# A decoder layer's two down projections, from plain k-tile sums to Strassen products

## The chip, the cores and the metric

One core of one Trainium2 chip runs the whole program in one launch. The time is the device time of one execution in microseconds (us); several runs give a median.

The engines, as the profile names them: PE is TensorE's matmuls (PEld its weight loads), DVE is VectorE, ACT is ScalarE, POOL is GpSimd, SP is SyncE, which here only issues DMAs. Each has its own queue and works through it in order; they wait for one another by semaphores. PE writes to PSUM, whose tiles DVE and ACT read; all else lies in SBUF or in DRAM.

## What is computed

One layer of a hybrid decoder for 1024 prompt and 64 sample positions, 1088 columns in all, width 1024, in fp32:

```
x = x + 1/2 * SwiGLU_1(rmsnorm(x))
h = rmsnorm(x);  z = h @ w_in
... three mixing branches (windowed attention, a recurrence, memory attention) ...
x = x + merged @ w_out
x = x + 1/2 * SwiGLU_2(rmsnorm(x))
y = rmsnorm(x)

def swiglu(x, w_gu, w_down):                 # d_model 1024, d_ff 2816
    gate, up = split(x @ w_gu, 2)
    return (silu(gate) * up) @ w_down
```

The change concerns the product with `w_down` in both SwiGLU blocks: 2816 x 1024 weights against 1088 columns.

## The kernel before

**Layout.** Everything is kept transposed: a tile has 128 rows (channels) and positions as its columns. d_ff is 22 k-tiles of 128 (`KF`), d_model 8 tiles (`KD`). The 1088 columns are taken either in three chunks of 352, 368 and 368 (`CH`), or in two halves (`tp`) of 544, each of two blocks of 272 columns (`TC`).

**A product in three matmuls.** Each fp32 operand is split into a coarse part and a rest (both fp32r). `mac3` (L262 to L264) issues three matmuls for each k-tile: coarse x coarse, coarse x rest, rest x coarse.

**Weights.** A plan (`make_plan`) lists all weight tiles in the order of use. `load` (L154) has SP fetch the next one, 128 x 1024 (512 KB), into one of four raw buffers (`wr`). `part` splits 128 x 512 of it: ACT copies the coarse part (L167), DVE subtracts it from the raw tile (L168). Seven split tiles (`ws`, `RING`) are the ring between them and PE. `ahead`, called inside `mac3`, has the next ones made as ring places come free.

**Gate stage** (`gate_up`). The up and gate products of a k-tile pair are Strassen's already (`quad`, `combined`): seven products of 272 columns, with sums of weight blocks on DVE and POOL (L183) and the results put together by `swiglu` (DVE L539, POOL L557, L561 and L506). The hidden tiles, silu(gate) x up, go to DRAM (`h_d`). The last two k-tiles (`ALONE`) are done for one half, then for the other; in between, `change` frees the first half's operands and starts the down stage's loads: `first_hidden` loads and splits hidden tiles 0 to 3, and in stage 1 `fetch_x` (L1654) loads the residual x straight into the accumulator.

**Down stage** (`down`, `down_tile`). The 22 k-tiles go in eleven pairs. For each pair, eight output tiles o times three chunks are six matmuls each into one PSUM bank; DVE adds the bank to the accumulator x in SBUF (L648). In stage 2 the first pair is copied by ACT (L646), and the residual is loaded and added to x by POOL (L1822) during the second pair. Hidden tiles are fetched by SP (L569) and split by ACT (L573, which also scales by 1/2) and DVE (L574). In the last pair the loop runs over the chunks outside, and `after` does each finished tile's share of what comes next: norm sums (L321), in stage 1 the split operands of the next product (L281, L282), in stage 2 the final norm.

The order of the instructions on each engine is the order in which the program issues them, as a scheduler lays them out; `tick` and `later` spread work of DVE, ACT and POOL between PE's tiles.

## Time and profile before

| | us |
|---|---|
| runs (3): median, lowest to highest | 2748.35, 2745.88 to 2750.64 |
| the profiled execution | 2746.11 |
| its span, first to last instruction | 2744.3 |
| TensorE's mean granted clock | 0.989 of full speed |
| PE, DVE, ACT, POOL busy | 2658.8, 1728.8, 910.3, 834.4 |
| matmuls of the down stages | 3168 |

The down stage of the first SwiGLU lies at 515 to 780 us of the span, that of the second at 2455 to 2723. Matmul records overlap their neighbours (a matmul's mean duration is longer than the distance to the next one's start), so a rate of PE is read from starts in a window. A few records can be missing.

### The profile page before, as it was taken

Reading aid. Unit: us, or ns where it says so; the run is one execution under the profiler, and the core shown is the slowest. Engines: PE = TensorE matmul, PEld = TensorE weight load, DVE = VectorE, ACT = ScalarE, POOL = GpSimd, SP = SyncE. Lnnn points to the kernel's source line nnn. Section 1 sums busy time; section 2 is a strip of 40 time slices with the busy share of each in tenths; the row PEclk is TensorE's granted clock in tenths of the full one; section 3 lists DMA queues with packets and bytes.
Section 4 is the critical chain, followed back from the end, with each engine's and each line's share of the span. In section 5 each row is a group of like instructions: output and inputs, shape, how many; then the busy total and the mean of one; then the engine's idle time right before and its main releaser. Section 6 shows DMA issues by size and latency. Waiting matters only on the chain.

```text
span 2744.3 us, 46291 instructions
## 1 busy us (share of the span) xinstructions
PE 2658.8 (97%) x18088; PEld 2578.8 (94%) x18088; DVE 1728.8 (63%) x3032; ACT 910.3 (33%) x1747; POOL 834.4 (30%) x751
## 2 busy tenths in 40 slices
PE   7999999999999999999989999999999999999997
PEld 7999999899999899989978889999999999999997
DVE  7766566777774433546577755863766666576776
ACT  6332323311153312323334543422542232242112
POOL 2365555200030000324353411231225555553003
PEclk9999999999999999999999999999999999999998
DMA  4222323522243342655544442754424455445221
GB/s 150 70 94 84 103 99 108 206 96 92 76 166 126 96 148 75 208 181 159 174 156 136 138 134 94 262 178 164 149 98 176 163 186 189 168 157 173 96 73 66
DMA packets 181403, 374.98 MB, mean 137 GB/s; under 512 B 21768, under 2 KB 116168, under 8 KB 180416
## 3 DMA queue, kind: packets, MB, share of 16 engines
q1 hardware_dynamic: 166464, 303.85, 33.7%
q0 software_dynamic: 2048, 43.65, 4.7%
q10 hardware_dynamic: 12672, 24.52, 2.4%
q8 instruction: 142, 2.33, 0.4%
q14 instruction: 77, 0.63, 0.1%
HBM read 305.59 MB, written 113.16 MB: 153 GB/s over the span
## 4 chain that ended last, share of the span: by engine, by line
PE 83%; DVE 10%; ACT 2%; issue 2%; DMA 2%; POOL 1%; SPq 0%; DVEq 0%; ACTq 0%; POOLq 0%
PE pg L262 9%; PE pg L264 9%; PE pg L263 9%; PE z L262 7%; PE z L263 7%; PE z L264 7%; PE pd L262 6%; PE pd L263 6%; PE pd L264 6%; DVE ws L168 2%; PE po L264 2%; PE po L263 2%; PE po L262 2%; PE o L814 1%; PE wo L262 1%
## 5 line engine op out<-in xcount | busy, mean ns | idle before, releaser
L262 PE MATMUL pg<-xo,ws 128*128 128x272 f32 x2512 | 730.3, 291 | 18.6 <-DVE uu L539 10.6
L264 PE MATMUL pg<-xo,ws 128*128 128x272 f32 x2512 | 727.0, 289 | 5.2 <-DVE ws L168 5.2
L263 PE MATMUL pg<-xo,ws 128*128 128x272 f32 x2512 | 726.7, 289 | 0.0
L167 ACT ACTIVATE ws<-wr 128x512 fp32r<-128x512 f32 (+1 forms) x550 | 324.9, 613 | 839.9 <-PE pd L264 363.9
L168 DVE TENSOR_TENSOR ws<-wr,ws 128x512 fp32r<-128x512 f32 (+1 forms) x550 | 439.4, 822 | 133.7 <-ACT ws L167 133.3
L262 PEld LDWEIGHTS pg<-xo,ws 128*128 128x128 f32 x2512 | 476.5, 190 | 21.3 <-DVE uu L539 12.8
L264 PEld LDWEIGHTS pg<-xo,ws 128*128 128x128 f32 x2512 | 476.4, 190 | 5.8 <-DVE ws L168 5.8
L262 PE MATMUL z<-xg,ws 128*128 128x368 f32 (+1 forms) x1392 | 478.9, 344 | 0.0
L263 PEld LDWEIGHTS pg<-xo,ws 128*128 128x128 f32 x2512 | 476.8, 190 | 0.0
L264 PE MATMUL z<-xg,ws 128*128 128x368 f32 (+1 forms) x1392 | 460.2, 331 | 0.0
L263 PE MATMUL z<-xg,ws 128*128 128x368 f32 (+1 forms) x1392 | 459.8, 330 | 0.0
L262 PE MATMUL pd<-h,ws 128*128 128x368 f32 (+1 forms) x1056 | 348.7, 330 | 3.7 <-DVE x L648 2.6
L263 PE MATMUL pd<-h,ws 128*128 128x368 f32 (+1 forms) x1056 | 346.8, 328 | 0.0
L264 PE MATMUL pd<-h,ws 128*128 128x368 f32 (+1 forms) x1056 | 345.9, 328 | 0.0
L648 DVE TENSOR_TENSOR x<-x,pd 128x368 f32<-128x368 f32 (+1 forms) x504 | 258.0, 530 | 137.6 <-PE pd L264 133.8
L262 PEld LDWEIGHTS z<-xg,ws 128*128 128x128 f32 x1392 | 265.2, 191 | 15.7 <-issue 14.2
L263 PEld LDWEIGHTS z<-xg,ws 128*128 128x128 f32 x1392 | 265.5, 191 | 1.4 <-issue 0.2
L264 PEld LDWEIGHTS z<-xg,ws 128*128 128x128 f32 x1392 | 264.1, 190 | 0.0
L262 PEld LDWEIGHTS pd<-h,ws 128*128 128x128 f32 x1056 | 199.3, 189 | 4.3 <-DVE x L648 2.9
L264 PEld LDWEIGHTS pd<-h,ws 128*128 128x128 f32 x1056 | 199.4, 189 | 0.0
L263 PEld LDWEIGHTS pd<-h,ws 128*128 128x128 f32 x1056 | 199.4, 189 | 0.0
L978 POOL TENSOR_TENSOR qb<-qb,kv 128x1024 f32<-128x1024 f32 x48 | 116.2, 2424 | 198.0 <-DMA qb<-qs_d 146.6
(297 smaller groups left out, 3705.0 us busy)
## 6 DMA issues: line engine op xcount, KB each, us to landing
wr<-in_w_gu_dram SPq DMA_DIRECT2D x96, 512.0 KB
wr<-in_w_in_dram SPq DMA_DIRECT2D x58, 512.0 KB
qb<-qs_d SPq DMA_DIRECT2D x48, 512.0 KB
h_d<-sl ACTq DMA_DIRECT2D x88, 272.0 KB
hr<-h_d SPq DMA_DIRECT2D x44, 544.0 KB
wr<-in_w_dn_dram SPq DMA_DIRECT2D x44, 512.0 KB
out_sk_dram<-in_cache_k_dram POOLq DMA_DIRECT2D x16, 1020.0 KB, 6.9
out_sv_dram<-in_cache_v_dram POOLq DMA_DIRECT2D x16, 1020.0 KB, 8.3
```

The lines of the kernel that those rows point to most:

```text
L167: nc.scalar.activation(spl[:, 0, :n], src, AF.Copy)
L168: nc.vector.tensor_tensor(out=spl[:, 1, :n], in0=src, in1=spl[:, 0, :n].bitcast(F32), op=OP.subtract)
L262: nc.tensor.matmul(out, wh, xh, start=start and i == 0, stop=False, **more)
L263: nc.tensor.matmul(out, wh, xl, start=False, stop=False, **more)
L264: nc.tensor.matmul(out, wl, xh, start=False, stop=i == n - 1, **more)
L648: nc.vector.tensor_tensor(out=xa, in0=xa, in1=ps[:, :n], op=OP.add)
L814: nc.tensor.matmul(po[:, e], pt[:, h, j * 128:(j + 1) * 128], z["vt"][:, kb[j], e], start=j == 0, stop=j == len(kb) - 1)
L978: nc.gpsimd.tensor_tensor(out=prev, in0=prev, in1=kk, op=OP.mult)
```

## The change

Twenty of the 22 k-tiles of each down stage are done in five groups of four (`DGROUPS`). A group is a 2 x 2 by 2 x 2 block product: weights in blocks of two k-tiles by four output tiles, hidden tiles in blocks of two k-tiles by 272 columns of both halves. Strassen's scheme (in Winograd's form) makes seven products of it, in the order `DOPS`.

- `downed` makes the split weights of the seven products, two tiles for each, from four raw tiles held at once. Sums of weight blocks are formed in place on POOL (L221 to L230 of the new file).
- `hidden_operand` splits an operand of 4 x 272 columns for each product (ACT, DVE L603) and forms sums of hidden blocks in place on POOL (L627). It is called two products ahead. `load_hidden` fetches two k-tiles in one DMA (L613).
- `down_groups` runs over 35 products. A product is four output tiles; each has 12 matmuls into a PSUM tile of two banks (544 columns in use), four of which exist. `sum_product` adds that tile to the product's own sum: products 5, 2, 4 and 3 straight in x, products 1, 6 and 7 in three further tiles (`sum`). In the first group ACT copies products 1, 5, 6 and 7; in products 6 and 2 (`DASIDE`) of all groups but the last, unless copied so, ACT copies the tile to SBUF (`et`) and POOL adds it (L736); all else is DVE's (L738).
- In the last group the seven sums are combined once, tile by tile, by DVE and POOL (`ends`, L686), in SBUF.
- The residual is loaded into x ahead of the first group in both stages (`residual`), but for one block of columns that product 5 writes first; that block comes apart (`late`) and is added in the last group.
- The last two k-tiles are left as they were (`down`); their hidden tiles are loaded and split during the last group.
- Weights of `w_down` come in plain rows, one k-tile of 128 x 1024 in each load.

```diff
-DOWN = [(k, 2, 512) for k in range(0, KF - 2, 2)] + [(KF - 2, 2, 1024)]
+DGROUPS = (KF - 2) // 4
+DOPS = (1, 5, 7, 6, 2, 4, 3)
+DASIDE = (6, 2)
...
+    def downed(self, name, raws):
+        tt = self.nc.gpsimd.tensor_tensor
+        blocks = [[r[:, a:a + 512] for r in (raws[q], raws[2 + q]) for a in (0, 512)] for q in range(2)]
...
+        for m in DOPS:
+            for q, (a11, a21, a12, a22) in enumerate(blocks):
+                put(m, q, {1: a11, 5: a21, 7: a11, 6: a11, 2: a12, 4: a22, 3: a12}[m])
+                if m == 1:
+                    if q == 0:
+                        tt(out=a11, in0=a11, in1=a21, op=OP.subtract)
+                    else:
+                        tt(out=blocks[0][1], in0=blocks[0][1], in1=blocks[0][3], op=OP.add)
+                        tt(out=a11, in0=a11, in1=a21, op=OP.subtract)
+                if (m, q) == (5, 0):
+                    tt(out=blocks[1][1], in0=blocks[1][1], in1=blocks[1][3], op=OP.add)
+                if m == 7:
+                    tt(out=a11, in0=a22, in1=a11, op=OP.subtract)
+                if m == 2:
+                    tt(out=a12, in0=a12, in1=a11, op=OP.subtract)
+                if q and m in (2, 3):
+                    self.load()
+                    self.load()
+                yield
...
+    def hidden_operand(self, n):
+        group, idx = divmod(n, 7)
...
+        self.split_hidden(self.hop[n], {1: b11, 5: b11, 7: b12, 6: b11, 2: b21, 4: b21, 3: b22}[m])
...
+        if m == 1:
+            less(b11, b12, b11)
+        if m == 5:
+            less(b12, b22, b12)
+        if m == 7:
+            less(b11, b22, b11)
+        if m == 2:
+            less(b21, b21, b11)
+            self.load_hidden(group + 1, 0)
+        if m == 3:
+            self.load_hidden(group + 1, 1)
...
-    def down(self, dn, pool, raws, after, residual=None):
-        for g, (k, nk, w) in enumerate(DOWN):
...
+    def down_groups(self, dn, sums, extra, src, last):
...
+        acc = {1: s1, 6: s6, 7: s7, 5: x11, 2: x00, 4: x10, 3: x01}
+        ends = {1: ((nc.vector, s6, s1), (nc.gpsimd, x00, s1)), 2: ((nc.gpsimd, x01, x11),),
+                3: ((nc.vector, x11, s7), (nc.gpsimd, x10, s7)), 4: ((nc.gpsimd, x11, "late"), (nc.vector, x01, s6)),
+                5: ((nc.vector, x10, s6),), 6: ((nc.gpsimd, x11, s6),)}
+        for n in range(7 * DGROUPS):
...
+            for o in range(4):
+                ps = self.bank("s", "pd")
+                for tp in range(2):
+                    self.mac3(ps[:, tp * 512:tp * 512 + TC],
+                              [(tuple(w[:, s, o * 128:(o + 1) * 128] for s in range(2)),
+                                (xo[:, 0, 2 * q + tp], xo[:, 1, 2 * q + tp])) for q, w in enumerate(ws)], steps=False)
+                self.sum_product(group, m, acc[m][o], ps.rearrange("p (t n) -> p t n", t=2)[:, :, :TC], end, extra)
+                if end:
+                    for eng, out, x in ends.get(idx, ()):
+                        tt(eng, out[o], late[:, o] if x == "late" else x[o])
+                if o < 2:
+                    if len(self.ready) + self.using < RING:
+                        self.make()
+                if o == 2:
+                    self.hidden_operand(n + 2)
...
+    def sum_product(self, group, m, acc, ps, end, extra):
+        nc = self.nc
+        if group == 0 and m in (1, 5, 6, 7):
+            nc.scalar.activation(acc, ps, AF.Copy)
+        elif m in DASIDE and not end:
+            t = extra("et")
+            nc.scalar.activation(t, ps, AF.Copy)
+            nc.gpsimd.tensor_tensor(out=acc, in0=acc, in1=t, op=OP.add)
+        else:
+            nc.vector.tensor_tensor(out=acc, in0=acc, in1=ps, op=OP.add)
```

What stands where, at three places. First DVE in the middle of the down stage 1 (`x` and `sum` are accumulators, `pd` is PSUM, `ws` split weights, `ho` a product's split hidden operand). Before:

```order
L648 TENSOR_TENSOR x_5535<-x_5535,pd_6165 128x352
L648 TENSOR_TENSOR x_5535<-x_5535,pd_6181 128x368
L648 TENSOR_TENSOR x_5535<-x_5535,pd_6189 128x368
L648 TENSOR_TENSOR x_5535<-x_5535,pd_6197 128x352
L648 TENSOR_TENSOR x_5535<-x_5535,pd_6205 128x368
```

After, in a middle group:

```order
L738 TENSOR_TENSOR x_5535<-x_5535,pd_7253 128x2x272
L171 TENSOR_TENSOR ws_7267<-wr_6978,ws_7267 128x512
L738 TENSOR_TENSOR x_5535<-x_5535,pd_7270 128x2x272
L171 TENSOR_TENSOR ws_7284<-wr_6976,ws_7284 128x512
L738 TENSOR_TENSOR x_5535<-x_5535,pd_7288 128x2x272
L603 SCALAR_TENSOR_TENSOR ho_7302<-hr_7015,ho_7302 128x1088
L738 TENSOR_TENSOR x_5535<-x_5535,pd_7306 128x2x272
```

and in the last group, with a combining sum (L686) behind each PSUM sum:

```order
L738 TENSOR_TENSOR x_5535<-x_5535,pd_7891 128x2x272
L686 TENSOR_TENSOR sum_5845<-sum_5845,sum_5844 128x544
L171 TENSOR_TENSOR ws_7907<-wr_7473,ws_7907 128x512
L738 TENSOR_TENSOR x_5535<-x_5535,pd_7910 128x2x272
L686 TENSOR_TENSOR sum_5845<-sum_5845,sum_5844 128x544
```

A product's four sums now alternate with two weight splits and one operand split; before, the splits of a pair stood between 24 sums.

Second POOL in stage 1. Before, nothing stands between the gate stage's last products and the norm sums of the last pair:

```order
L557 TENSOR_TENSOR uu_5747<-uu_5747,rbc 128x544
L506 TENSOR_TENSOR sl_5787<-sl_5787,uu_5747 128x544
L321 TENSOR_TENSOR acc_8038<-acc_8038,td_8052 128x352
```

After, from a middle group's product 2 on (`et` is ACT's copy of a PSUM tile, `wr` raw weights, `hr` raw hidden tiles):

```order
L736 TENSOR_TENSOR x_5535<-x_5535,et_7117 128x2x272
L736 TENSOR_TENSOR x_5535<-x_5535,et_7140 128x2x272
L221 TENSOR_TENSOR wr_6976<-wr_6976 128x512
L736 TENSOR_TENSOR x_5535<-x_5535,et_7160 128x2x272
L736 TENSOR_TENSOR x_5535<-x_5535,et_7181 128x2x272
L223 TENSOR_TENSOR wr_6976<-wr_6976,wr_7123 128x512
L224 TENSOR_TENSOR wr_6978<-wr_6978 128x512
L226 TENSOR_TENSOR wr_6978<-wr_6978,wr_7125 128x512
L627 TENSOR_TENSOR hr_7015<-hr_7015 128x4x272
```

Four more such L736 rows stand right ahead; the weight sums of the next group, L223 among them, stand behind all eight.

Third SP's queue at the opening of stage 1. Before:

```order
L154 DMA wr_5580<-in_w_dn_dram 128x1024
L569 DMA hr_5536<-h_d 128x1088
L569 DMA hr_5538<-h_d 128x1088
L154 DMA wr_5582<-in_w_dn_dram 128x1024
L1654 DMA x_5535<-in_x_dram 128x1088 x8
L569 DMA hr_5686<-h_d 128x1088
L154 DMA wr_5725<-in_w_dn_dram 128x1024
```

After:

```order
L157 DMA wr_5586<-in_w_dn_dram 128x1024
L613 DMA hr_5542<-h_d 128x2x1088
L613 DMA hr_5544<-h_d 128x2x1088
L157 DMA wr_5588<-in_w_dn_dram 128x1024
L681 DMA x_5535<-in_x_dram 128x1088 x4
L679 DMA x_5535<-in_x_dram 128x2x272 x4
L157 DMA wr_5724<-in_w_dn_dram 128x1024
L157 DMA wr_5726<-in_w_dn_dram 128x1024
L679 DMA late_7815<-in_x_dram 128x2x272 x4
```

All four hidden tiles of the first group now stand ahead of x, and the third and fourth weight tile behind it.

## Rows read from the trace of the kernel before

**Rows 1.** The page, busy us (share of the span), instructions of each engine.

```profile
PE 2658.8 (97%) x18088; PEld 2578.8 (94%) x18088; DVE 1728.8 (63%) x3032; ACT 910.3 (33%) x1747; POOL 834.4 (30%) x751
```

**Rows 2.** Windows: length, then PE, PEld, DVE, ACT, POOL busy, clock, DMA, GB/s.

```profile
560.00:720.00 160.00, 160.00 (x977) 160.00 (x976) 113.79 (x203) 30.18 (x42) 0.00 (x0) 1.00 0.27 89
350.00:400.00 50.00, 50.00 (x402) 50.00 (x401) 29.54 (x50) 13.68 (x24) 26.52 (x22) 1.00 0.23 79
480.00:502.00 22.00, 19.19 (x149) 18.53 (x148) 21.88 (x30) 10.21 (x17) 12.12 (x8) 1.00 0.66 254
```

**Rows 3.** The tile pd: durations min/median/max in ns, one of three matmul lines.

```profile
L262 PE MATMUL pd<-h,ws x1056: 317/330/508, 515.7 to 2722.4; 128*128 128x352 f32 x166, 128*128 128x368 f32 x10
```

**Rows 4.** Groups by line and shape, DVE, 520 to 760 us: busy us, mean ns.

```profile
L648 DVE TENSOR_TENSOR x<-x,pd 128x368 f32<-128x368 f32 x160 | 84.9, 537 | 50.4 <-PE pd L264 50.4
L648 DVE TENSOR_TENSOR x<-x,pd 128x352 f32<-128x352 f32 x85 | 44.0, 519 | 16.9 <-PE pd L264 16.9
L168 DVE TENSOR_TENSOR ws<-wr,ws 128x512 fp32r<-128x512 f32 x41 | 26.4, 685 | 3.3 <-ACT ws L167 3.3
L574 DVE SCALAR_TENSOR_TENSOR h<-hr,h 128x1088 fp32r<-128x1088 f32 x18 | 23.1, 1284 | 0.0
```

**Rows 5.** The same view, DVE, gate stage, 200 to 460 us.

```profile
L539 DVE TENSOR_TENSOR uu<-pg,uu 128x272 f32<-128x272 f32 x25 | 11.0, 442 | 15.0 <-PE pg L264 13.7
...
L183 DVE TENSOR_TENSOR s<-s,wr 128x512 f32<-128x512 f32 x12 | 8.3, 693 | 0.4
```

**Rows 6.** The same view, POOL, 200 to 460 us and 520 to 760 us.

```profile
L183 POOL TENSOR_TENSOR wr<-wr,s 128x512 f32<-128x512 f32 x13 | 16.7, 1287 | 111.5 <-DVE ws L168 111.5
...
L506 POOL TENSOR_TENSOR sl<-sl,uu 128x544 f32<-128x544 f32 x1 | 1.4, 1357 | 1.1 <-issue 1.1
```

**Rows 7.** The same view, ACT, 520 to 760 us.

```profile
L167 ACT ACTIVATE ws<-wr 128x512 fp32r<-128x512 f32 x41 | 23.7, 624 | 193.9 <-PE pd L264 193.9
L573 ACT ACTIVATE h<-hr 128x1088 fp32r<-128x1088 f32 x18 | 18.9, 1098 | 0.0
```

**Rows 8.** Timeline of DVE: start us, us, what.

```profile
498.83 0.69 DVE L168 TENSOR_TENSOR ws<-wr,ws 128x512 fp32r<-128x512 f32 x1
499.43 1.28 DVE L574 SCALAR_TENSOR_TENSOR h<-hr,h 128x1088 fp32r<-128x1088 f32 x1
500.63 0.43 DVE L539 TENSOR_TENSOR uu<-pg,mu 128x272 f32<-128x272 f32 x1
```

**Rows 9.** Timelines of DVE and of POOL where both work.

```profile
480.09 1.78 DVE L168 TENSOR_TENSOR ws<-wr,ws 128x512 fp32r<-128x512 f32 x1
...
482.15 1.49 DVE L168 TENSOR_TENSOR ws<-s,ws 128x512 fp32r<-128x512 f32 x1
...
479.52 1.80 POOL L183 TENSOR_TENSOR wr<-wr,wr 128x512 f32<-128x512 f32 x1 [1.58 <-DVE s L183]
481.29 1.80 POOL L506 TENSOR_TENSOR sl<-sl,uu 128x544 f32<-128x544 f32 x1
...
2517.32 2.13 DVE L574 SCALAR_TENSOR_TENSOR h<-hr,h 128x1088 fp32r<-128x1088 f32 x1
...
2515.76 2.54 POOL L1822 TENSOR_TENSOR x<-x,xr 128x1088 f32<-128x1088 f32 x1 [1.29 <-DVE h L574]
```

**Rows 10.** Groups by line and shape, DVE, 467 to 510 us.

```profile
L168 DVE TENSOR_TENSOR ws<-wr,ws 128x512 fp32r<-128x512 f32 x18 | 19.6, 1087 | 0.9 <-ACT ws L167 0.9
```

**Rows 11.** The chain of waits, 500 to 512 us, and a window.

```profile
502.06 7.93 DMA hr<-h_d
...
508.00:516.00 8.00, 4.92 (x25) 4.70 (x26) 5.43 (x9) 3.78 (x5) 0.03 (x1) 0.76 0.97 371
```

**Rows 12.** Windows at the end of stage 1 and in stage 2.

```profile
2520.00:2530.00 10.00, 7.41 (x45) 7.09 (x44) 8.35 (x14) 0.76 (x2) 6.90 (x3) 1.00 0.59 211
760.00:790.00 30.00, 25.86 (x159) 24.95 (x158) 29.33 (x55) 21.05 (x43) 18.88 (x18) 0.98 0.41 147
```

More of the change, by code (lines that the diff above doesn't have):

```diff
@@ L211, in make @@
             name, raw, n = self.raw()
+            if name[0] == "%":
+                self.rest = self.downed(name, [raw] + [self.raw()[1] for _ in range(3)])
+                next(self.rest)
+                return
             if name[0] == "*":
@@ L578, in raw_tiles @@
[L578 to L587 removed]
+        nc.scalar.activation(h[:, 0], src, AF.Copy, scale=0.5)
+        nc.vector.scalar_tensor_tensor(h[:, 1], src, 0.5, h[:, 0].bitcast(F32), op0=OP.mult, op1=OP.subtract)
@@ L640, in down_tile @@
+    def down_tile(self, ws, ks, o, c):
         nc = self.nc
@@ L1660, in emit @@
     ps0.close()
+    last, K.h = range(4 * DGROUPS, KF), {}
+    with ExitStack() as es:
+        K.banks(es, "psum1s", s=4)
+        pool = right(es, "sums1")
+        K.down_groups("w_dn1", lambda m: pool.tile([128, 4, 2, TC], F32, name=f"sum{m}"), sized(pool, late=1, hr=2, et=3),
+                      lambda o: K.i["x"][o], last)
+    ops1.close()
     K.banks(ps1, "psum1", mm=6, t=2)
```

181 lines of the change are left out of this document (106 added, 75 removed).

## The prediction

> **What bounds the kernel now.** First the page's busy shares: TensorE is busy for 97% of the span, VectorE (DVE) for 63% [rows 1]. Then the windows of the two stages that the change rewrites. In the down stage PE is busy without a gap, 977 matmuls in 160 us, DVE for 114 of them, GpSimd (POOL) for none; in the gate stage, whose products are already Strassen's with 272 columns, 402 matmuls in 50 us, also without a gap, with POOL busy for 27 [rows 2]. So both stages are paid in matmul starts: 160/977 = 163.8 ns for a mean of 363 columns, 50/402 = 124.4 ns for 272. A down stage is 1584 matmuls (3 x 1056 in two stages, [rows 3]).
>
> What the reader should keep beside this is the idle POOL of the down stage. DVE has room there only because POOL does nothing: a weight split takes 0.685 us in that stage [rows 4] and 1.087 us in the stretch ahead of it [rows 10], where POOL is busy for 12.1 of 22 us and DVE for 21.9 [rows 2].
>
> **What the change takes from PE.** Twenty of 22 k-tiles go from 1440 matmuls of 363 columns to 35 products of 48 matmuls of 272 columns, 1680; the last two k-tiles keep 144. After: 1680 x 124.4 + 144 x 163.8 ns = 209.0 + 23.6 = 232.6 us. Before: 1584 x 163.8 ns = 259.4 us. Saved: 26.8 us a stage, 53.6 us in all, if PE never waits. One group of seven products is then 41.8 us of PE, one product 5.98 us, one PSUM tile (12 matmuls) 1.5 us, and four such tiles are all the PSUM there is: PE waits when DVE is more than some 4.5 us late.
>
> **What it adds, in a middle group (three a stage), against 41.8 us.**
> DVE: 20 sums of a 544-column PSUM tile. No row has that width; 272, 352 and 368 columns take 0.44, 0.52 and 0.54 us [rows 4, 5], about 1.05 ns a column, so 0.72 us (estimate). Fourteen weight splits at 0.685 (eight before) and seven operand splits of 1088 elements at 1.284 us (four before) [rows 4]. Back to back, instructions of DVE follow each other some 0.08 us closer than their durations: the split at 498.83 is followed at 499.43, that of 499.43 at 500.63 [rows 8], so 0.60 and 1.20 us, and 0.65 for a tile. Sum 20 x 0.65 + 14 x 0.60 + 7 x 1.20 = 29.8 us.
> POOL, idle here before: eight weight sums of 512 at 1.287, eight sums of 544 at 1.357 [rows 6], four sums of 1088 at 2.54 us [rows 9]. Sum 31.4 us.
> ACT: 14 x 0.62 + 7 x 1.10 [rows 7] and eight PSUM copies, which by its row for 512 elements are some 0.65 each: 21.6 us, hidden.
> So each engine alone fits into 41.8 us. Together DVE and POOL may not. At 479.52 POOL's sum of 512 takes 1.80 us instead of 1.29, and DVE's split, issued at 480.09, takes 1.78 instead of 0.69: it works from 481.18 on, when POOL has worked for 1.1 us. At 482.15 the split begins 1.2 us into a POOL sum of 544; at 2517.32 the operand split (2.13 us) begins 2.4 us into POOL's sum of 1088 [rows 9]. DVE's instructions on two SBUF operands and POOL's take turns; those that read PSUM (0.43 us on either side of such a wait) do not. Turns of a middle group: POOL 8 x 1.1 + 8 x 1.2 + 4 x 2.4 = 28.0, DVE 14 x 0.60 + 7 x 1.20 = 16.8 us, together 44.8 us: 3.0 more than PE needs. Bounds: nothing, if the four PSUM tiles and the weights made two products ahead carry it (the sums on PSUM, 13 us of DVE, can run beside POOL), and 8.2 us with whole durations in place of turns (18.6 + 31.4 = 50.0). I take 3.0, the sum nearest to the rows of the turns: 6 x 3.0 = **18 us**.
>
> The first group of a stage has ACT for 16 of its tiles and four POOL sums fewer; its turns are 40.0 us: nothing.
>
> **The last group** pays for combining once. DVE gets 28 PSUM sums, 16 SBUF sums of 544 (by the 512-element sum at 0.69 us [rows 5] some 0.73, 0.65 apart), 13 weight splits and seven operand splits (two of them the plain tiles'): 28 x 0.65 + 16 x 0.65 + 13 x 0.60 + 7 x 1.20 = 44.8 us without any wait. POOL gets 20 sums of 544 beside three of 1088 and four of 512. Turns: DVE 26.6, POOL 20 x 1.2 + 3 x 2.4 + 4 x 1.1 = 35.6, less the last four sums, which can fall behind the group (4.8): 57.4 us, 15.6 over 41.8. Bounds: 3.0 (DVE's own work) and 22.3 (whole durations, 29.6 + 39.9 - 5.4 = 64.1). In stage 1 what follows has DVE busy for 29.3 of 30 us [rows 12], so nothing is won back; in stage 2 DVE has no operand for a next layer to split, and I give back 3 us. **15.6 + 12.6 = 28.2 us.**
>
> **The openings.** In stage 1 the chain of waits stands for 7.93 us on the load of a hidden tile that is queued behind eight loads of x (4.46 MB); PE is then 61% busy at 0.76 of the clock [rows 11], that is, partly at 1.2 instead of 2.4 GHz. The change puts the hidden tiles ahead of x. But SP's queue now has two weight tiles behind x, and POOL's first sum of weights needs the third tile: up to it the queue holds 2.23 + 0.52 + 3.34 + 0.52 = 6.6 MB, as much as before up to the hidden tile (1.11 + 0.52 + 4.46 + 0.56 = 6.65 MB). On DVE the split that needs this sum stands among the last gate products' PSUM sums, as the hidden tile's split did. So the stall stays, and the fourth tile comes 0.52 MB / 371 GB/s = 1.4 us later: +1.5 (bounds -7, the whole stall, and +5). In stage 2, where x isn't loaded so early, five new POOL sums, two of 1088 and three of 512, meet a DVE that is late anyway: by their turns they cost it between nothing and 2 x 2.4 + 3 x 1.1 = 8.1 us; I let PE wait 2.
> Gone: stage 2's adding of x on POOL; PE was busy for 7.41 of 10 us there while it ran, at full clock [rows 12]: **-2.6 us**.
> DMAs: about 4.2 MB a group in 42 us, 100 GB/s against 89 now [rows 2]; the queue is idle for most of the stage, so nothing.
>
> **Sum**: -53.6 + 18 + 28.2 + 3.5 - 2.6 = -6.5 us on the profiled execution's 2746.1 us: 2739.6, say **2740 us**. That execution is 2.2 us under the median of the three runs and inside their range.
>
> **Rule against trace.** The rows above show DVE going on before POOL's record ends. The Trainium skill, SBUF — State Buffer, "SBUF: two separate sides", says that the pair of ports which both share is an exclusive lock, held for the whole instruction, against DVE instructions with two SBUF inputs. The trace agrees on the lock and on which instructions it hits, and differs on the hold (1.1 of 1.29 us); by the page's hold the time would be that of the second rival.
>
> **Rivals.**
> (1) *The cover holds.* The middle groups run at PE's pace the last loses half of the 15.6 us, some 8, and the openings cost 2: -53.6 + 3 + 16 + 2 - 2.6 = -35 us, 2711 (the 3 is half a microsecond for each middle group). For it: DVE and POOL are below 76% each in a middle group, DVE's order alternates PSUM and SBUF instructions, and PSUM carries four tiles. Against it: the port's sum is above PE's in every middle group.
> (2) *The port is held for whole instructions*, as both engines' durations would have it: middle groups of 50.0 us, last ones 64.1: -53.6 + 49 + 41.6 + 3.5 - 2.6 = +38 us, 2784. For it: 1.087 us in place of 0.685 for the mean split beside a POOL that is busy for little more than half of the time [rows 2, 10]. Against it: the turns read in rows 9.
> (3) *The seam.* The slower side by one mechanism: eight sums of ACT's copies stand on POOL ahead of the sum that makes the fifth product's weights of the next group. Cluster and one weight sum: 8 x 1.36 + 1.29 us, six DVE turns between them (4 x 0.6 + 2 x 1.2), from 2.1 us into the first of its two products, ends at about 19 us, 7 us after those 12 us. ACT's copy, then DVE's split wait for it, and behind that split on DVE stand the PSUM sums; PE runs out of tiles 9 us after the seam. Up to some 7 us of lateness is covered; each further one is paid at four seams a stage. At 3 us each: +24, so 2764. It decides from 10 us of lateness on.
> That the products don't shrink as said is not to be feared: PE's program has 480 matmuls more, 2 x (1824 - 1584).
>
> **Chances.** Forecast (2725 to 2753) 0.45; cover holds (below 2725) 0.24; seam (2753 to 2772) 0.19; port for whole instructions (above) 0.12. A measurement of this kernel tells 0.2%, 5.5 us, from no change: faster is below 2742.9, slower above 2753.8. Faster: 0.24 + 0.6 x 0.45 = 0.51. Within: 0.18, the rest of the forecast's band. Slower: 0.31. Range 2706 to 2772: it leaves out the lower third of the first rival and most of the second. The forecast's own range is 2725 to 2753.
>
> **What would show it.** PE's windows: a middle group near 45 us, the first at 42, the last at 57, with PE's waits put down to DVE's sums on pd. DVE's weight splits at about 1 us in place of 0.685, POOL above 60% in the down stages. If the middle groups take 42 us the port is no limit and rival 1 holds; if 50, rival 2; if the waits bunch at the fifth product's weights with POOL as releaser, rival 3. The forecast is wrong if the last group costs as little as the others, or if the 272-column matmuls start more than 124.4 ns apart where PE has no wait.

## The result and the profile after

The kernel after takes 2827.56 us (median of 4 runs, 2825.50 to 2828.31), the kernel before on the same chip 2749.49 (4 runs, 2745.88 to 2752.51): a ratio of 1.0283, 95% interval 1.0265 to 1.0301. The change makes the kernel 78 us slower. The forecast was 2740 us with a range up to 2772; both its sign and its range were wrong.

The page of after, the line that answers to [rows 1], and the chain that ended last by engine (before: PE 83%, DVE 10%, POOL 1%):

```profile
PE 2650.1 (94%) x18568; PEld 2556.0 (90%) x18568; DVE 1872.9 (66%) x2890; ACT 1020.5 (36%) x1901; POOL 1211.9 (43%) x959
PE 66%; DVE 19%; issue 5%; POOL 4%; ACT 3%; DMA 2%; SPq 0%; DVEq 0%; ACTq 0%; POOLq 0%
```

PE has 480 matmuls more, as the prediction said, and is busy for 9 us less. But 17% of the span has left PE in the chain, nearly all of it to DVE, POOL and to issue.

The windows of after, one for each of the five groups of stage 1 (PE, PEld, DVE, ACT, POOL busy, clock, DMA share, GB/s). The row to hold beside them is the first of [rows 2], where PE is busy without a gap:

```profile
526.00:572.00 46.00, 45.20 (x340) 44.80 (x341) 27.45 (x25) 25.68 (x41) 26.30 (x16) 0.95 0.44 150
572.00:623.00 51.00, 44.40 (x334) 43.42 (x333) 44.08 (x42) 20.44 (x30) 37.00 (x20) 0.97 0.25 86
623.00:674.00 51.00, 44.86 (x339) 43.91 (x337) 44.10 (x42) 20.43 (x30) 36.99 (x20) 0.97 0.25 86
674.00:725.00 51.00, 46.23 (x338) 45.26 (x337) 43.19 (x42) 20.34 (x30) 37.03 (x20) 0.93 0.25 86
725.00:793.00 68.00, 54.52 (x343) 51.90 (x342) 67.86 (x67) 17.11 (x24) 52.13 (x27) 0.82 0.12 39
```

Each row is one group, 336 matmuls; the counts differ from that because a window's edges cut through the neighbours. By the starts of their matmuls a middle group takes 51 us and the last 67, where 336 matmuls without a wait take 42.3 (6.04 us a product, 125.8 ns a matmul; the prediction took 124.4). In the last group DVE is busy from end to end. From the starts of the matmuls, stage by stage:

| us of the span | before | after | difference |
|---|---|---|---|
| stage 1: up to the first down matmul | 515.7 | 526.1 | +10.4 |
| its 20 k-tiles | 237.8 | 266.4 | +28.6 |
| its two plain k-tiles | 26.4 | 30.8 | +4.4 |
| stage 2: first gate matmul to first down matmul | 484.3 | 495.2 | +10.9 |
| its 20 k-tiles | 244.0 | 267.2 | +23.2 |
| its two plain k-tiles | 25.4 | 27.7 | +2.3 |
| all else | | | +2.4 |

Together +82.2 us, the difference of the two spans. The stretch between the stages, 1189.2 us in before, runs the same instructions in every kernel below and lies between 1184.6 and 1194.4 us there: a single run's time carries some 5 us of that, so experiments are compared by their stages. One profiled execution is left out of all this, that of the run with 16 shared sums, which had a granted clock of 0.67 and took 3540 us; its other ten took 2741.85 to 2752.36.

DVE's groups by line, 560 to 725 us, to hold beside [rows 4]:

```profile
L171 DVE TENSOR_TENSOR ws<-wr,ws 128x512 fp32r<-128x512 f32 x45 | 59.8, 1335 | 20.8 <-ACT ws L170 20.5
L603 DVE SCALAR_TENSOR_TENSOR ho<-hr,ho 128x1088 fp32r<-128x1088 f32 x23 | 45.2, 1967 | 3.7 <-ACT ho L602 3.7
L738 DVE TENSOR_TENSOR x<-x,pd 128x544 f32<-128x544 f32 x41 | 28.7, 707 | 0.0
```

The split of 512 has gone from 685 to 1335 ns, the operand split from 1284 to 1967. The 544-column sum on PSUM takes 707, as estimated. What reads two SBUF operands pays, what reads PSUM doesn't.

**The seam of two groups**, POOL at 598 to 618 us, then the rows of ACT and DVE that wait for it:

```profile
598.66 7.71 POOL L736 TENSOR_TENSOR sum<-sum,et 128x544 f32<-128x544 f32 x4
606.33 4.24 POOL L736 TENSOR_TENSOR x<-x,et 128x544 f32<-128x544 f32 x2
610.54 1.74 POOL L221 TENSOR_TENSOR wr<-wr 128x512 f32<-128x512 f32 x1
612.24 2.66 POOL L736 TENSOR_TENSOR x<-x,et 128x544 f32<-128x544 f32 x2
614.86 1.26 POOL L223 TENSOR_TENSOR wr<-wr,wr 128x512 f32<-128x512 f32 x1
...
616.15 0.63 ACT L170 ACTIVATE ws<-wr 128x512 fp32r<-128x512 f32 x1 [6.83 <-POOL wr L223]
...
616.81 1.08 DVE L171 TENSOR_TENSOR ws<-wr,ws 128x512 fp32r<-128x512 f32 x1 [5.05 <-ACT ws L170]
617.82 0.71 DVE L738 TENSOR_TENSOR x<-x,pd 128x544 f32<-128x544 f32 x1
```

Eight sums of ACT's copies and one of weights stand ahead of L223 on POOL. ACT waits 6.83 us for it, DVE 5.05 us for ACT, and the sum on PSUM that would free a tile for PE stands behind that wait. PE, 615 to 623.2 us, in the two windows that follow: three matmuls in 4 us, and then the clock at 0.59 for the next 4:

```profile
615.00:619.00 4.00, 0.42 (x3) 0.42 (x4) 2.19 (x3) 1.63 (x2) 3.92 (x3) 1.00 0.00 0
619.00:623.20 4.20, 4.20 (x23) 4.20 (x22) 4.20 (x4) 1.53 (x3) 2.56 (x2) 0.59 0.00 0
```

That product, the seventh of its group, takes 12.1 us in place of 6.04; the next group's second takes 8.4. The same stands in all three middle groups of both stages (9.9 to 13.1 and 7.4 to 9.4).

**The last group**, DVE and POOL at 759 to 767 us:

```profile
759.35 1.82 DVE L171 TENSOR_TENSOR ws<-wr,ws 128x512 fp32r<-128x512 f32 x1
761.10 0.71 DVE L738 TENSOR_TENSOR sum<-sum,pd 128x544 f32<-128x544 f32 x1
761.73 1.24 DVE L686 TENSOR_TENSOR x<-x,sum 128x544 f32<-128x544 f32 x1
762.89 1.83 DVE L171 TENSOR_TENSOR ws<-wr,ws 128x512 fp32r<-128x512 f32 x1
...
760.58 7.12 POOL L686 TENSOR_TENSOR x<-x,sum 128x544 f32<-128x544 f32 x4
767.67 7.72 POOL L686 TENSOR_TENSOR x<-x,late 128x544 f32<-128x544 f32 x4
```

POOL goes from one combining sum to the next without a pause, 1.8 to 1.93 us each in place of 1.357; between two of them one DVE instruction on SBUF gets through.

**The opening**, the same instructions in stage 1 and stage 2 (POOL, and what waits for it):

```profile
511.99 3.52 POOL L627 TENSOR_TENSOR hr<-hr,hr 128x1088 f32<-128x1088 f32 x1
515.48 1.72 POOL L223 TENSOR_TENSOR wr<-wr,wr 128x512 f32<-128x512 f32 x1
517.23 0.63 ACT L170 ACTIVATE ws<-wr 128x512 fp32r<-128x512 f32 x1 [5.76 <-POOL wr L223]
...
2495.97 3.52 POOL L627 TENSOR_TENSOR hr<-hr,hr 128x1088 f32<-128x1088 f32 x1
2499.45 1.72 POOL L223 TENSOR_TENSOR wr<-wr,wr 128x512 f32<-128x512 f32 x1
2501.20 0.63 ACT L170 ACTIVATE ws<-wr 128x512 fp32r<-128x512 f32 x1 [5.75 <-POOL wr L223]
```

To about a hundredth of a microsecond the same, though only stage 1 has the loads of x in the queue.

### The profile page after: what moved, and what is told of

Same layout as the page of the kernel before. It is cut to its first block, busy times and chain, and to the rows that moved or that the text cites. A ratio compares the mean times of both kernels' runs of the same rounds, so it can differ in the third digit from the quotient of the medians.

```text
span 2826.5 us, 47236 instructions
## 1 busy us (share of the span) xinstructions
PE 2650.1 (94%) x18568; PEld 2556.0 (90%) x18568; DVE 1872.9 (66%) x2890; ACT 1020.5 (36%) x1901; POOL 1211.9 (43%) x959
## 4 chain that ended last, share of the span: by engine, by line
PE 66%; DVE 19%; issue 5%; POOL 4%; ACT 3%; DMA 2%; SPq 0%; DVEq 0%; ACTq 0%; POOLq 0%
PE pg L296 9%; PE pg L298 9%; PE pg L297 9%; PE z L296 7%; PE z L297 7%; PE z L298 7%; DVE ws L171 5%; DVE x L738 2%; DVE ho L603 2%; PE po L298 2%; PE po L297 2%; PE po L296 2%; PE pd L296 1%; PE pd L297 1%; PE pd L298 1%
## 5 line engine op out<-in xcount | busy, mean ns | idle before, releaser
L296 PE MATMUL pg<-xo,ws 128*128 128x272 f32 x2512 | 730.9, 291 | 25.4 <-DVE uu L573 15.1
L171 DVE TENSOR_TENSOR ws<-wr,ws 128x512 fp32r<-128x512 f32 (+1 forms) x610 | 575.3, 959 | 181.7 <-ACT ws L170 179.1
L170 ACT ACTIVATE ws<-wr 128x512 fp32r<-128x512 f32 (+1 forms) x610 | 364.1, 614 | 664.3 <-PE pg L298 322.7
L296 PEld LDWEIGHTS pg<-xo,ws 128*128 128x128 f32 x2512 | 477.2, 190 | 28.2 <-DVE uu L573 16.7
L296 PE MATMUL pd<-ho,ws 128*128 128x272 f32 x1120 | 340.9, 304 | 81.1 <-DVE x L738 44.2
L298 PE MATMUL pd<-ho,ws 128*128 128x272 f32 x1120 | 333.6, 298 | 0.0
L297 PE MATMUL pd<-ho,ws 128*128 128x272 f32 x1120 | 333.0, 297 | 0.0
L296 PEld LDWEIGHTS pd<-ho,ws 128*128 128x128 f32 x1120 | 221.0, 197 | 94.9 <-DVE x L738 51.6
L297 PEld LDWEIGHTS pd<-ho,ws 128*128 128x128 f32 x1120 | 222.0, 198 | 0.0
L298 PEld LDWEIGHTS pd<-ho,ws 128*128 128x128 f32 x1120 | 221.3, 198 | 0.0
L186 POOL TENSOR_TENSOR wr<-wr,s 128x512 f32<-128x512 f32 x42 | 55.0, 1311 | 311.5 <-DVE ws L171 311.5
```

The source lines that it names most:

```text
L170: nc.scalar.activation(spl[:, 0, :n], src, AF.Copy)
L171: nc.vector.tensor_tensor(out=spl[:, 1, :n], in0=src, in1=spl[:, 0, :n].bitcast(F32), op=OP.subtract)
L186: eng.tensor_tensor(out=out, in0=x, in1=y, op=op)
L296: nc.tensor.matmul(out, wh, xh, start=start and i == 0, stop=False, **more)
L297: nc.tensor.matmul(out, wh, xl, start=False, stop=False, **more)
L298: nc.tensor.matmul(out, wl, xh, start=False, stop=i == n - 1, **more)
```

## The experiments

All but the last two give the time of one profiled execution; the kernel before took 2746.6 to 2749.6 us beside them. Group lengths are from the starts of matmuls.

**Is the opening's stall the DMA queue's?** x's residual is asked for after the first group's weights.

```diff
-    operand_pool([pool] * 3), lambda: K.residual(lambda o: K.i["x"][o]))
+    operand_pool([pool] * 3), lambda: None)
...
     pool = right(es, "sums1")
+    K.residual(lambda o: K.i["x"][o])
```

> The changed kernel, but stage 1 issues the loads of the residual x where the down groups begin, behind all four weight tiles of the first group, as stage 2 does. Theory of the prediction (the weight tiles stand behind x in SP's queue): the first down matmul of stage 1 comes at 513 to 516 us in place of 526.1, and the span is about 10 us shorter, 2816. Rival (the opening waits for a chain POOL, ACT, DVE: POOL's sum of weights stands behind its sum of hidden blocks, DVE's split waits for it and the gate stage's PSUM sums stand behind that): stage 2 opens 11 us late too, without x in the queue, so nothing changes, first matmul within 2 us of 526 and span within 3 us of 2826.

Measured: 2827.22 us; the first down matmul at 525.25 in place of 526.15, and the 0.9 us between them arise early in the gate stage. It isn't the queue behind x. The rival's chain POOL, ACT, DVE is left; the runs without POOL's sums and with some of them on DVE bear on it below.

**Where do the eight sums of ACT's copies hurt?** They are moved to the third and fourth product of a group, away from the seam.

```diff
-DASIDE = (6, 2)
+DASIDE = (7, 6)
```

> The changed kernel with ACT's copies and POOL's sums (DASIDE) for products 7 and 6 in place of 6 and 2, so that the eight POOL sums of a middle group end one product earlier; the port's work is the same but for the first group, where POOL then gets none of them. Seam theory (POOL's queue is late for the fifth product's weight sums, DVE stands behind them): the seventh product of groups 1 to 4 falls from 12.1 us to 6 to 7, middle groups from 51 to 45 or 46, span about 33 us shorter, 2793. Port theory (DVE and POOL take turns and their sum is more than PE needs): middle groups stay at 50 to 52, only stalls move to other products; span within 8 us of 2826.

Measured: 2811.39 us. The seventh product falls from 12.1 to 6.1 us, but the two products behind the sums now take 7.7 each: middle groups 46.5 to 49.8, mean 49.0, in place of 51.1. The place of the sums at the seam is a part of the loss; most of it moves with them.

**POOL altogether.** All its sums in the down groups are left out.

```diff
-        tt = self.nc.gpsimd.tensor_tensor
+        tt = lambda **k: None
...
-            self.nc.gpsimd.tensor_tensor(out=out, in0=x, in1=y, op=OP.subtract)
...
-            nc.gpsimd.tensor_tensor(out=acc, in0=acc, in1=t, op=OP.add)
...
                     for eng, out, x in ends.get(idx, ()):
+                        if eng is nc.gpsimd:
+                            continue
```

> Leaves out every sum on POOL in the down groups: the sums of weight blocks and of hidden blocks, the sums of ACT's copies and POOL's part of the combining. All matmuls, splits and DVE's sums stay. If POOL (by its queue or by the port) is the cause of all the loss: every group takes PE's 42.3 us, the last 44 to 46, stage 1 opens at 516; about 52 + 52 us less in the groups and 10 + 11 at the openings: span 2700 to 2710. If DVE by itself is too slow for PE: middle groups stay above 45 and the last above 55, span above 2740.

Measured: 2699.47 us, a middle and the last group of stage 1 in windows:

```profile
600.00:642.00 42.00, 42.00 (x336) 42.00 (x336) 31.08 (x42) 19.32 (x30) 0.00 (x0) 1.00 0.31 104
684.00:728.00 44.00, 42.97 (x338) 42.35 (x337) 42.56 (x62) 15.15 (x21) 0.00 (x0) 1.00 0.18 61
```

PE has no gap in a middle group, the last takes 44.06 us, the first down matmul starts at 515.07 us and the split of weights is back at 687 ns. The loss in the groups and at the openings hangs on POOL's sums, but for 1.8 us a last group, and PE's saving is real: 48 us below before. The plain k-tiles' loss doesn't: they take 31.1 and 29.2 us here, against 26.4 and 25.4 before.

**The combining sums.** They are left out, DVE's and POOL's.

```diff
-                    for eng, out, x in ends.get(idx, ()):
-                        tt(eng, out[o], late[:, o] if x == "late" else x[o])
+                    pass
```

> Leaves out the combining sums of the last group (on DVE and POOL, ends). If they are the last group's price: it falls from 67.3 us to 45 to 48 (a middle group without a next one's seam), span about 40 to 44 us shorter, 2784. If the last group is slow from what it inherits from the seam ahead and from the plain tiles' splits: it stays above 55.

Measured: 2772.87 us; the last groups are 47.1 and 44.8 us in place of 67.2 and 67.7, the middle ones unchanged (49.8 to 52.1). The plain k-tiles are back at 26.9 and 25.5 us: what they lost comes from the combining sums just ahead of them, and, by the run without POOL's sums, from DVE's own part of these too.

**Port or queue?** POOL's sums of ACT's copies and its part of the combining are left out; in the place of each stand two fills, 1.1 us together, which read nothing.

```diff
-            nc.gpsimd.tensor_tensor(out=acc, in0=acc, in1=t, op=OP.add)
+            nc.gpsimd.memset(t, 0.0)
+            nc.gpsimd.memset(t, 0.0)
...
                     for eng, out, x in ends.get(idx, ()):
+                        if eng is nc.gpsimd:
+                            eng.memset(out[o], 0.0)
+                            eng.memset(out[o], 0.0)
+                            continue
```

> GpSimd's sums of ACT's copies, and its half of the combining sums in the last group, are left out; in the place of each stand two fills of a 544-column tile with zeros, so that part of the result is not formed. The trace of before has such fills at 0.525 us for 512 and 0.95 us for 1024 columns, so GpSimd is held in the same places for about 1.1 us in place of 1.2, but reads nothing from SBUF. Theory A, the shared port: VectorE's weight splits beside these fills are back at 0.69 us, its combining sums at 0.72, and the last groups fall from 67 us to what VectorE's own work asks for, 45 to 48. In the middle groups only the delay in GpSimd's queue is left: the seventh product stays above 6.04 us, the group at 45 to 48 us in place of 51. Time 2770 to 2785. Theory B, GpSimd's queue alone (its order, who waits for whom): the middle groups stay at 50 to 51 and the last ones above 60, time above 2810.

Measured: 2761.37 us. POOL's fills at 598 to 601 us follow each other without a pause, and DVE's splits beside them:

```profile
599.54 0.55 POOL L740 MEMSET et<- 128x544 f32 x1
600.15 0.55 POOL L741 MEMSET et<- 128x544 f32 x1
600.65 0.55 POOL L740 MEMSET et<- 128x544 f32 x1
601.26 0.55 POOL L741 MEMSET et<- 128x544 f32 x1
...
599.71 0.69 DVE L171 TENSOR_TENSOR ws<-wr,ws 128x512 fp32r<-128x512 f32 x1 [0.94 <-ACT ws L170]
601.05 0.69 DVE L171 TENSOR_TENSOR ws<-wr,ws 128x512 fp32r<-128x512 f32 x1 [0.66 <-ACT ws L170]
```

They take 0.69 us, and the fills are not slowed. Middle groups 44.1 to 46.5 us, last groups 52.0 and 51.1 (above the 45 to 48 expected: POOL's weight and hidden sums are still there). The shared port it is, and most of the queue at the seam as well: from its first fill to the end of L223 the cluster takes 11.5 us here and 17.5 in after. Some 2 of these 6 us aren't the port's, since two fills (1.1 us) are shorter than a sum that nothing slows (1.357). By the Trainium skill, SBUF — State Buffer, "SBUF: two separate sides", DVE instructions with two SBUF inputs meet the lock only against a GpSimd instruction that reads SBUF; this run agrees.

**Fewer holds.** First the sums that ACT copied for POOL go to DVE, then POOL's 20 combining sums of a last group too, then the two hidden differences that are made ahead of a first group.

```diff
-DASIDE = (6, 2)
+DASIDE = ()
```

> The sums on PSUM of the third and fourth... of products 6 and 2 go to VectorE as those of the others do, so ACT's copies and GpSimd's eight sums a group are gone from the middle groups. VectorE then has 28 x 0.65 + 14 x 0.60 + 7 x 1.20 = 35.0 us of work in a group, GpSimd eight weight sums and four of 1088. Theory A (port and seam were these eight sums): turns on the port 18.4 + 16.8 = 35.2 us, nothing stands ahead of the weight sums, the middle groups fall from 51 to 42.3 to 44, the last groups stay at 67; time 2827 - 6 x 8 = 2780. Theory B (VectorE becomes the bound: 35 us of its own and its waits for 18 us of GpSimd): middle groups of 47 or more, time above 2800.

Measured: 2779.64 us; middle groups 43.1 to 47.1 us, mean 44.7, last ones 67.5.

```diff
-                        tt(eng, out[o], late[:, o] if x == "late" else x[o])
+                        tt(nc.vector, out[o], late[:, o] if x == "late" else x[o])
```

> As the run without ACT's copies, and the 20 combining sums that GpSimd has in the last group go to VectorE too. VectorE's own work there is 28 x 0.65 + 36 x 0.65 + 13 x 0.60 + 7 x 1.20 = 57.8 us. Theory A (the last group is 67 us long because each of GpSimd's 20 sums stands in VectorE's way for 1.2 us): the group becomes VectorE's own 58 to 60 us, 8 us less a stage, time some 16 us below that of the run without the copies, 2764. Theory B (GpSimd's sums ran beside VectorE's and cost little): 13 us more a stage, the groups reach 75 us or more, time above 2790.

Measured: 2780.14 us. The last groups fall to 62.8 and 61.3, 5 to 6 us less, above the 58 to 60 expected. The time shows none of it: 3.4 us go to stage 2's plain k-tiles, the rest is the stretch between the stages, 9.4 us longer here with the same instructions. Neither theory's time was met.

```diff
-            self.nc.gpsimd.tensor_tensor(out=out, in0=x, in1=y, op=OP.subtract)
+            (self.nc.vector if n < 2 else self.nc.gpsimd).tensor_tensor(out=out, in0=x, in1=y, op=OP.subtract)
```

> As the run with all combining sums on VectorE, and the two differences of hidden tiles (1088 columns) that are made ahead of a stage's first group go to VectorE, where they take 1.2 us each. In the trace of after the first of them, 3.52 us on GpSimd, stands ahead of the sum of weights for which ACT waits 5.76 us and VectorE 1.48. Theory A (GpSimd's queue makes the opening's stall): that sum comes 3.5 us earlier, the openings lose 3 to 5 us each, time 6 to 10 us below the run before this one. Theory B (VectorE, late in the gate's last tiles, is the cause): VectorE is 2.4 us later, the openings grow by about that, time 5 us above it.

Measured: 2775.34 us; the openings are 1.7 us shorter each, about half of the least expected.

**Who makes the weight sums?** On the kernel of the last run, with x's residual behind the weights: all on DVE, or those beside products 1 and 5.

```diff
-        tt = self.nc.gpsimd.tensor_tensor
+        tt = self.nc.vector.tensor_tensor
```

> As the run with the first hidden differences on VectorE (2775.3 us); all eight sums of weights of a group go to VectorE too, and x's residual is asked for behind the first group's weights. GpSimd keeps only the four differences of hidden tiles a group. VectorE's own work in a middle group is 35.0 + 8 x 0.60 = 39.8 us, and GpSimd's four differences hold the port for 9.6. Theory A (what is left of the loss, 2 to 4 us a middle group and 5 us an opening, is the time for which a weight split waits for a GpSimd sum that the port has stretched): openings lose 3 to 4 us each, middle groups 43, the time is 10 to 15 us lower, 2760 to 2765. Theory B (VectorE is full): its 39.8 us and the waits for four holds of 2.4 us exceed 42.3, the middle groups stay at 45 or grow to 47, the time is 2775 or more.

```diff
+            tt = (self.nc.vector if m in (1, 5) else self.nc.gpsimd).tensor_tensor
             for q, (a11, a21, a12, a22) in enumerate(blocks):
```

> As the run before this one, but only the four weight sums made beside products 1 and 5 are on VectorE; the other four stay on GpSimd. VectorE's own work in a middle group is 37.4 us. In the run that this stands on, the second product of a group is the one that waits (8.4 us against 6.04). Theory A (it waits for weights whose sums GpSimd makes late): the second product falls to 6.0 to 6.5 us, middle groups to 42.3 to 43, openings lose 3 to 4 us each, time 2755 to 2762. Theory B (VectorE's order of work is the limit there): the second product keeps its 8 us, the groups stay at 45, and the time within 5 us of 2775.

Measured: 2773.88 and 2772.73 us. The openings are 1.0 and 1.3 us shorter in the first, 2.4 and 2.8 in the second; the middle groups have a mean of 45.2 us in both (44.8 in the run that they stand on): the weight sums aren't what holds them up.

**Is DVE full, or are the last holds too long?** On the first of these two, the hidden differences are left out from the third product on, so that POOL has nothing; on the second, each is made in two halves.

```diff
+            if n < 2:
+                self.nc.vector.tensor_tensor(out=out, in0=x, in1=y, op=OP.subtract)
```

> As the run with all weight sums on VectorE, and the differences of hidden tiles are left out from the third product of a stage on (so the products use tiles that were not subtracted), so GpSimd has nothing left in the down groups while VectorE keeps its 39.8 us a middle group. Theory A (the 3 us that are left in a middle group are waits of VectorE's splits for GpSimd's 2.4 us holds): splits of weights at 0.69 us, middle groups 42.3 to 42.8, last groups 60 to 61 (3 x 2.4 us of holds less than 63.7), time about 2753. Theory B (VectorE is full at 39.8 us in an order that PE's four tiles don't even out): middle groups stay at 45 or more, time 2770.

```diff
+            for a in (0, 2):
+                self.nc.gpsimd.tensor_tensor(out=out[:, a:a + 2], in0=x[:, a:a + 2], in1=y[:, a:a + 2], op=OP.subtract)
```

> As the run with four of the weight sums on VectorE (2772.7 us), but each difference of hidden tiles on GpSimd is made in two halves of 544 columns, which hold the port for 1.2 us each in place of 2.4 for the whole, so that a split of VectorE can go between them. Theory A (what hurts is how long one hold is, since PE's four tiles cover 4.5 us of lateness): middle groups 45.2 fall to 43 to 44, time 2758 to 2766. Theory B (the sum of the holds counts, however cut): no change, within 4 us of 2772.7 in the same stages.

Measured: 2741.38 and 2747.82 us. Without the differences a middle group takes 42.3 us and the last 55.7 (60 to 61 expected), so DVE's 39.8 us fit. With halves the middle groups of stage 1 are 42.28 us and those of stage 2 42.4 to 42.7, in place of 45.2, better than expected, though POOL is busy longer than with whole ones (a middle group of each). With whole differences, the run with four weight sums on DVE:

```profile
561.00:605.00 44.00, 42.76 (x340) 42.54 (x339) 43.97 (x52) 14.30 (x21) 16.80 (x8) 1.00 0.29 99
```

With halves:

```profile
563.00:605.00 42.00, 42.00 (x336) 42.00 (x335) 41.95 (x53) 15.07 (x22) 20.28 (x12) 1.00 0.31 104
```

How long one hold is decides here, not how much time the holds take together.

**Is that the whole of it?** The kernel after as it is, every POOL sum of the down groups in two halves.

```diff
+        def tt(out, in0, in1, op):
+            for a in (0, 256):
+                self.nc.gpsimd.tensor_tensor(out=out[:, a:a + 256], in0=in0[:, a:a + 256], in1=in1[:, a:a + 256], op=op)
...
+            for a in range(2):
+                nc.gpsimd.tensor_tensor(out=acc[:, a], in0=acc[:, a], in1=t[:, a], op=OP.add)
```

(the hidden differences and POOL's combining sums likewise)

> The kernel after the change as it is, with one difference: every sum that GpSimd makes in the down groups (of weights, of hidden tiles, of ACT's copies, of the combining) is made in two halves, of 256, 544 and 272 columns. The sum of GpSimd's holds of the port is the same or somewhat more, the longest hold is half as long. Theory A (how long one hold is decides, since VectorE waits for at most one hold a time): middle groups fall from 51 us to 43 to 46, the last groups from 67 to about 60, the openings lose 3 to 5 us each, time 2765 to 2785. Theory B (the sum of the holds decides, as the prediction's turns had it): middle groups stay at 50 to 52, the last ones at 67 or above, time 2825 to 2840.

Measured: 2802.97 us, 24 us below after and between the two theories. In the middle groups the second product falls from 7.4 to 9.4 us to 6.0 to 6.7, and the last groups to 61.9 and 62.5, but the seventh product grows to 11.6 to 15.9, and the middle groups are 49.9 in the mean; the openings are only 1.0 us shorter. Shorter holds free DVE; the sums of ACT's copies, 1.03 us for each half, lengthen POOL's queue ahead of the weight sums (at the first seam between middle groups 18.4 us up to the sum that ACT waits for, in place of 17.5). So there are two costs: DVE's wait for a hold, which halves cure, and POOL's queue at the seam, which they make worse.

**The combining sums, shared.** On the kernel with halves of the hidden differences, some of them go back to POOL in halves of 272 columns: 12 of 36; 16 (with those beside the seventh product, `idx` 6); or only the eight beside the last two products (`idx in (5, 6)`), whichever engine had them.

```diff
+                        if idx in (1, 3, 4) and eng is nc.gpsimd:
+                            for a in range(2):
+                                tt(eng, out[o][:, a], y[:, a])
+                        else:
+                            tt(nc.vector, out[o], y)
```

> As the run with the hidden differences in halves (2747.8 us), but 12 of the 36 combining sums of a last group (those into the first, third and fourth quarter of x that GpSimd had in the change) are GpSimd's again, in halves of 272 columns. VectorE's own work in a last group is 57.8 - 12 x 0.65 = 50.0 us. Theory A (halves fit between VectorE's sums on PSUM): last groups 53 to 55 in place of 59.5 and 61.3, time 2735 to 2740, below the kernel before. Theory B (each half still costs VectorE its hold, 24 x 0.6 = 14.4 us): last groups 60 to 65, time 2750 or more.

> As the run in which GpSimd has 12 of the combining sums in halves (2745.3 us), and it has the last four of a group (into the fourth quarter of x, beside the seventh product) too. VectorE has 4 x 0.65 = 2.6 us less, and these sums lie beside its sums on PSUM of the plain tiles, which don't want the port. Theory A (VectorE's own work sets the end of a last group): the last group and the plain tiles behind it take 2 to 3 us less a stage, time 2739 to 2743, ratio to before 0.997 to 0.999. Theory B (the holds cost VectorE as much as the sums would): within 2 us of 2745.3, ratio 0.999 to 1.000.

> As the run with the hidden differences in halves and all combining sums on VectorE (2747.8 us), but the eight combining sums beside the sixth and the seventh product are GpSimd's, in halves of 272 columns, and no others. VectorE has 8 x 0.65 = 5.2 us less at the end of a last group, just ahead of the operand split for which PE waits 4.6 us in the plain tiles. Theory A: 3 to 5 us less a stage, time 2738 to 2742, ratio 0.996 to 0.998. Theory B (the holds cost VectorE what the sums would, or GpSimd is late for the plain tiles' sums on the same part of x): within 2 us of 2747.8 or above, ratio 1.000 or more.

Measured: with 12, 2745.32 us, last groups 58.1 and 59.5 in place of 59.5 and 61.3, between the two theories: under 2 us for 7.8 us of DVE's work, so most of it came back as waits. With 16 the ratio to before is 0.9999 (0.9989 to 1.0010), no gain. With the last eight alone 0.9983 (0.9974 to 0.9992), last groups 57.5 and 58.7, stage 2's plain k-tiles 2.2 us shorter (median of 11 runs 2744.12, before 2748.01 in 21): the only version with the whole result that is measurably below before, by 4 to 5 us, less than expected. PE's saving of 58.8 us is still lost, in its trace, in the last groups (15.2 and 16.5 us above PE's pace), at the openings (5.3 and 6.7, counted as in the table above) and in the plain k-tiles (5.8 and 3.4).

## Why the prediction was wrong

Three steps failed. The sum of turns was taken for the price of a middle group, at 3.0 us (measured 8.8), with POOL's late weight sums at the seam held to be covered. In the last group's sum of turns 23 us were taken as hidden, and 13 were. The openings were priced at 3.5 us, stage 1's by the DMA queue, where POOL's sums set both, at 18.1.

| term, both stages, us | predicted | measured |
|---|---|---|
| 20 k-tiles before, at 163.8 ns a matmul | 471.7 | 481.8 |
| ten groups at PE's pace (41.8, 42.3) | 418 | 423 |
| six middle groups, above that pace | +18 | +53.1 |
| two last groups | +28.2 | +50.3 |
| two first groups | 0 | +7.2 |
| two openings | +3.5 | +18.1 |
| two plain stages | 0 | +6.7 |
| gone in stage 2 (x added by POOL) | -2.6 | in the first row |
| early in the first gate stage, and elsewhere | 0 | +5.6 |

The measured column is 423 - 481.8 + 53.1 + 50.3 + 7.2 + 18.1 + 6.7 + 5.6 = +82.2 us. (Of stage 1's +10.4, 3.2 arise early in its gate stage, in the run without POOL's sums too, and not in that without the combining sums, which has the same gate stage: they aren't the change's. They are in the last row.) The first row shows that the 20 k-tiles of before took 10.1 us longer than at PE's pace, of which the prediction named 2.6.

**What held.** The number of matmuls, PE's pace (125.8 for 124.4 ns), the 544-column sum (707 ns for an estimated 720), DVE fitting alone (the run without POOL's sums: 42.3 us a middle group, 44.06 the last, for 44.8 estimated), the port as the main risk, and the hold of some 1.1 us.

**The middle groups** were mis-sized by the sum of turns, 44.8 us, which was held against PE's 41.8 as if the rest of DVE's work could lie beside POOL's holds at will. (POOL's own sum in it, 31.4 us, adds up to 31.3.) With that rest, DVE's 13 us on PSUM, both engines have 57.8 us; the group took 51.1, so by this sum about half of the 13 overlapped. The reason against free overlap is order: DVE takes its instructions in turn, and a PSUM sum behind a split that waits for POOL waits too. The runs showed that in two ways: shorter holds with the same work free PE, and the same sums elsewhere cost elsewhere. Nor is the loss spread over the group, as a sum of turns has it: of the 53.1 us some 34 lie at the seventh products and 14 at the second, and the fourth to sixth all take 6.0 us.

**Rival 3 had the mechanism**, and its chain was read row for row in after: POOL's cluster, L223, ACT's copy, DVE's split, the PSUM sum behind it, PE out of tiles some 9 us after the seam. The cluster took 17.5 us against the rival's 17.0, with two weight sums (L221 and L223) where the rival had one. What was wrong is its start: 5.6 us into the two products in place of 2.1, since a hidden difference of 2.54 us stands ahead of it on POOL and itself waits for DVE. So the lateness was 11 us, not 7, and cost 6.1 us at the seventh product, not 3. The 2.4 us at the second product are another cost, which no rival named: they stay when ACT's copies and their sums are gone (6.8 to 9.5 us there), and go when the hidden differences are made in halves. By these runs they are waits for a whole hold of 2.4 us.

**Rival 2** had 50.0 us for a middle group, and "if 50, rival 2" was one of the signs named. The 51.1 us meet that number by luck: beside POOL's sums back to back the split takes 1.82 us, its 0.69 and a hold of some 1.1, so the hold isn't the whole 1.357, and the loss lies at two products. Its time, 2784, wasn't met either.

**The last group** was 10 us longer than its 57.4. DVE's own work was put at 44.8, POOL's holds at 35.6: of their sum, 80.4, 23.0 were to be hidden (DVE's 18.2 on PSUM, and 4.8 behind the group), and 12.9 were. Its rows show why: POOL is always ready with the next sum, so a split waits for nearly a whole hold, 1.82 us in place of 0.69; a sum on SBUF behind one on PSUM, which runs during the hold, still takes 1.24 in place of some 0.72. What was put at nothing for the plain k-tiles, +6.7, is DVE's work on the combining sums, which reaches into them: without these sums it is gone.

**The openings** failed by their step, not only their size. The cause was put to the queue behind x; putting x behind the weights changes nothing, and stage 2, without x, loses the same. Counted from the same gate matmul, some 105 us ahead of the down stage, to the first down matmul, stage 1's opening takes 105.6 us in before, 112.6 in after and 101.9 without POOL's sums; stage 2's takes 101.6, 112.6 and 101.8. So the stall that was said to stay in stage 1 is gone once POOL's sums are (3.7 us), and these cost 10.8 us in either stage. The "five new POOL sums" were named for stage 2 alone and priced at 2 of their 8.1 us; the measured 10.9 are above even that bound. Nor did the prediction see that DVE's waits here hold up the last gate tiles' PSUM sums (in stage 2, 5.8 of the 10.9 us lie before the last gate matmul). With some of POOL's sums on DVE the openings are shorter; how the rest divides between port and order there was not taken apart. The first groups, put at nothing, lost 3.2 and 4.0 us, nearly all at their first product, behind the opening, and at their seventh.

**The clock** was not in the sum: 0.974 in place of 0.989 over the span. At the seam the row at 0.59 has 21 matmuls starting in 4.2 us (two of its 23 began before), 200 ns apart in place of 125.8: some 1.5 of the 6.1 us there. It is a second price of each stall, not a cause.

## What to carry to other kernels

Before work goes to an idle GpSimd, count the VectorE instructions beside it that read two SBUF operands: each may wait for a GpSimd instruction's hold (here 1.1 to 2.4 us), and all that stands behind it on VectorE, reads of PSUM too, waits with it. Place GpSimd's sums by their queue (what urgent sum stands behind a bulk of others?). Cut long ones: holds of 2.4 us cost PE time here, though PSUM's four tiles were estimated to cover 4.5, and holds of 1.2 nearly none in a middle group. But don't cut a bulk of sums that stands ahead of an urgent one. Check a sum of busy times against order: two engines that both fit by their own busy time took 51 us together where neither needed 32.

## What was not expected of the hardware

- Cutting four GpSimd sums of 1088 columns in two raised GpSimd's busy time (16.8 in 44 us to 20.3 in 42) and still took 2.8 us off a middle group (45.2 to 42.4 in the mean).
- GpSimd's fills of SBUF don't slow VectorE's two-operand instructions (0.69 us) nor are slowed by them (0.55), while GpSimd's sums go from 1.357 to 1.93 and the splits from 0.69 to 1.8.
- Where both engines always had work, they alternated one for one: four GpSimd sums and four VectorE instructions on SBUF between 760.6 and 767.7 us, in the last group of after.
- After about 4 us in which TensorE did three matmuls the clock fell to 0.59 in the mean of the next 4.2 us; the longer stalls of the last group leave 0.82 over its 68 us.
